# Token sums written unrounded by ScalarE, two modulation vectors moved to VectorE, in a two-layer mLSTM / SGU / conv backbone

## The chip, the cores and the metric

The kernel runs on one core of one Trainium2 chip. The metric is the device time of one execution in microseconds (us). The core has a matrix engine (TensorE, PE in the profile), a vector engine (VectorE, DVE), a scalar engine (ScalarE, ACT), GpSimd (POOL) and a queue engine that issues DMAs (SyncE, SP). Each engine works through its own list of instructions in order and waits on semaphores for the others. Matrix products are accumulated in PSUM, which has eight banks here (the kernel calls them `ps`).

## The reference

The reference is a backbone of two layers over 512 latent tokens and 256 context tokens with 1024 features. Cut to what matters here:

```
for l in range(2):
    mod  = silu(c)     @ w_mod[l] + b_mod[l]      # six vectors: sh1, sc1, g1, sh2, sc2, g2
    modc = silu(c_ctx) @ w_mod[l] + b_mod[l]      # the same for the context tokens
    p = (rmsnorm(x, norm1_g) * (1 + sc1) + sh1) @ w_in[l] + b_in[l]
    y = concat(mlstm(p), spatial_gating(p), conformer_conv(p))
    x = x + g1 * (y @ w_out[l])
    h = rmsnorm(x, norm2_g) * (1 + sc2) + sh2     # "the second norm"
    gate, up = split(h @ w_gu[l])
    x = x + g2 * ((silu(gate) * up) @ w_down[l])
out = rmsnorm(x, final_g)
```

The context tokens go through the same weights with their own modulation; in the second layer only what the latent tokens read of them is computed.

## The kernel before

**Data.** Activations stand with features on the 128 partitions: `xT[:, k, t]` is feature block k (of 8) and token t. Every large product is made from three passes of a rounded format (fp32r): each operand is split into a rounded part `hi`, written by ACT, and the remainder `lo`, written by DVE, and PE adds hi x hi, hi x lo and lo x hi. `HH[:, 0]` and `HH[:, 1]` hold the `hi` and `lo` of the normalised activations.

**Weights.** SP loads 512 KB tiles into four `raw` buffers, in the order in which the program uses them. ACT and DVE split a weight tile (lines 374, 376, 457, 334), and the raw buffer is free after that. A tile of modulation weights is not split; it is free when the engine that uses it is done with it.

**Modulation vectors.** There are two ways to make one of the six vectors of a layer. `mod_steps` makes a vector in eight steps on PE: each step multiplies a 512 KB tile with the two conditioning columns in four matmuls with 32 output rows and 256 columns (line 650). `modh_steps` makes it in two halves of four steps on DVE: each step multiplies two blocks of 512 columns by a conditioning value per partition and adds them up (`macc`; line 724 the first, line 727 the others), for each of the two conditioning columns, four operations per tile; at the end of a half PE sums over the partitions (line 737: eight matmuls, recorded as 16). Both end in `mod_fin`, which transposes the result. Before, layer 0 makes vectors 2, 3, 4 and 5 by `mod_steps`, and layer 1 makes all of its six by `modh_steps` while layer 0's feed-forward part runs. Vector 2 is the gate of the first residual, 3 and 4 are the shift and the scale of the second norm.

**The second norm.** `norm` forms `nt`, the normalised and scaled row of block k, on DVE (line 893); `norm_lo` adds the shift: ACT writes `hi` (line 868), DVE writes `lo` (line 870). It goes through k = 0 to 7, for one group of tokens after the other (layer 0: context 256, latent 512; layer 1: latent 256 and 256).

**The feed-forward part.** The hidden columns of the gate and up projections are made in two ways. The first two (layer 0) or three (layer 1) hidden blocks are "plain" columns: `tiles` over all eight k, with three passes (lines 528 to 530). All the others come as pairs by one level of a fast 2 x 2 product: seven products of quarter size (`pair_steps`, lines 1889 to 1891, PSUM tiles `bA`, `bB`, `bC`) in place of eight. Each product multiplies a combination of weight quarters (formed on DVE, line 420) with a quarter of the activations or with one of four combinations of its quarters, the **token sums**. The activations' quarters are blocks 0 to 3 and 4 to 7 by the first and second half of the tokens. `t_forms` makes the token sums, for k = 0 to 3: it waits for the norm's rows k and k + 4, adds `hi` and `lo` back together into a buffer `tf` (line 1783, 1536 or 1024 columns), combines the quarters in four operations (lines 1786 to 1792), and splits the result again on ACT (line 1796) and DVE (line 1798). There are two `tf` buffers, so that k = 2 and 3 wait for k = 0 and 1. The first pair's second product of activations uses all four token sums.

**Memory.** Twelve `slot` buffers serve the mLSTM part, the convolution, the gating and then the feed-forward part. `ffn_memory` waits for all twelve and hands out the `tf` buffers, the places of the split token sums and places for hidden blocks.

**The order of the work.** The program is written as threads, and a planner (`Plan`) runs them once when the kernel is built: each thread asks for an engine with an estimated cost, and the planner gives each engine to the thread that could start first, on a tie the one with the smaller priority number. The order in which it hands out the engines is the order of each engine's instructions; on the chip it is fixed. PE's list follows the list of steps, into which `spread` mixes modulation steps evenly. Weight splits have priority 0, the norm 0.5, the token sums 0.55 to 0.58, hidden rows 0.6, mLSTM work 0.9 to 3, the convolution's taps and the additions of `modh_steps` 4.

Of the kernel before, what the change touches and what calls it, by code (L numbers as in the profile page):

```python
# [168 lines left out]
def W(ev):  # L169
    return ("w", ev)  # L170
# [53 lines left out]
def backbone(ctx, tc, xT_d, cT_d, wmod_d, wb_d, wgv_d, wv_d, wout_d, wgu_d, wd_d, sw_d, sb_d, cv_d, rv_d, id_d, mk_d, out_d):  # L224
# [639 lines left out]
    def norm_lo(tag, l, which, t, k, grp):  # L864
        n, t0, g, h, o = grp["n"], grp["t0"], grp["g"], grp["h"], grp["off"]
        sh = MODC[l][:, (0, 3)[which], k, g:g + 1]
        yield ACT(n)
        act.activation(h[:, 0, k, o:o + n], t, AF.Identity, bias=sh)
        yield STT(n)
        dve.scalar_tensor_tensor(h[:, 1, k, o:o + n], t, sh, h[:, 0, k, o:o + n].bitcast(F32), ALU.add, ALU.subtract)  # L870
        release("pb")
        fire(ev("h", l, which, t0, k))

    def norm(l, which, grp, stat=None):
# [11 lines left out]
        for k in range(KD):  # L886
# [7 lines left out]
            if k == KD - 1:  # L894
                release("slot" if early else "ps")
# [26 lines left out]
    def layer(l):  # L922
# [765 lines left out]
        if not last:  # L1688
            steps = steps[:first] + spread(steps[first:], [m for v in (2, 3, 4) for m in mod_steps(l, v)])
# [29 lines left out]
        nout = len(steps)  # L1719
# [11 lines left out]
        def spawn_ffn():  # L1731
            spawn(ffn_memory(), 0.5)
            spawn(t_forms(), 0.55)
            return
            yield
# [16 lines left out]
        def ffn_memory():  # L1752
            yield A("slot", 12)
            st["tf"] = [slot([P, 2, 2, HM], "tf") for _ in range(2)]
            sl = [slot([P, 3, 512], "ffn", F32R) for _ in range(10)]
            flat = [x.rearrange("p a b -> p (a b)") for x in sl]
            if not last:
                for k in range(4):
                    TF[k] = tuple(flat[2 * k + w].rearrange("p (a t) -> p a t", a=4) for w in range(2))
                more_hid([tuple(flat[8 + i][:, w * NT:(w + 1) * NT].rearrange("p (a b) -> p a b", a=2) for w in range(2)) for i in range(2)])  # L1760
            else:
                for k in range(4):
                    TF[k] = (HB[:, k // 2, 4 * (k % 2):4 * (k % 2) + 4, :], flat[k][:, 0:1024].rearrange("p (k t) -> p k t", k=4))
                more_hid(piece_hid([x[:, 2] for x in sl[0:4]] + [x[:, i] for x in sl[4:] for i in range(3)]))
# [5 lines left out]
        def t_forms():  # L1770

            yield W(E("ffnmem"))
            tf = st.pop("tf")

            def form(k, f):
                for g in (gl, gg):
                    for kk in (k, k + 4):
                        yield W(ev("h", l, 1, g["t0"], kk))
                if k >= 2:
                    yield W(E("T", k - 2))  # L1780
                rows = [HH[:, w, :, 0:NT].rearrange("p (a b) t -> p a b t", a=2)[:, :, k] for w in range(2)]
                yield DVE2(4 * HM)
                dve.tensor_tensor(f.rearrange("p a b t -> p a (b t)"), rows[0].bitcast(F32), rows[1].bitcast(F32), ALU.add)
                fire(E("tread", k))
                yield DVE2(HM)
                dve.tensor_tensor(f[:, 0, 0], f[:, 0, 0], f[:, 0, 1], ALU.subtract)
                yield DVE2(HM)
                dve.tensor_tensor(f[:, 0, 1], f[:, 1, 1], f[:, 0, 1], ALU.subtract)
                yield STT(HM)
                dve.scalar_tensor_tensor(f[:, 1, 1], f[:, 0, 0], -1.0, f[:, 1, 1], ALU.mult, ALU.subtract)  # L1790
                yield STT(HM)
                dve.scalar_tensor_tensor(f[:, 1, 0], f[:, 1, 1], -1.0, f[:, 1, 0], ALU.mult, ALU.subtract)
                hi, lo = TF[k]
                ff = f.rearrange("p a b t -> p (a b) t")
                yield ACT(4 * HM)
                act.copy(hi, ff)
                yield DVE2(4 * HM)
                dve.tensor_tensor(lo, ff, hi.bitcast(F32), ALU.subtract)  # L1798
                fire(E("T", k))
                if k >= 2:  # L1800
                    release("slot")

            for k in range(4):
                spawn(form(k, tf[k % 2]), 0.55 + 0.01 * k)
            yield W(E("T", 2))
            yield W(E("T", 3))
            yield A("slot", 2)
            x = [slot([P, 3, 512], "ffn", F32R) for _ in range(2)]
            if not last:
                x = [y.rearrange("p a b -> p (a b)") for y in x]  # L1810
                more_hid([tuple(y[:, w * NT:(w + 1) * NT].rearrange("p (a b) -> p a b", a=2) for w in range(2)) for y in x])
            else:
                more_hid(piece_hid([y[:, i] for y in x for i in range(3)]))
# [6 lines left out]
        def more_room():  # L1820
            for k in range(4):
                yield W(E("tread", k))
# [258 lines left out]
        steps.append(([], lambda: spawn_ffn()))  # L2081
        np_ = NPLAIN[l]
        steps += tiles([gu_col(i) for i in range(2 * np_)], gl, gg, KD, hsrc, lambda k, g: ev("h", l, 1, g["t0"], k), wide=True, ahead=AHEAD[2])
# [176 lines left out]
```

## Time and profile before

The device time is 1557.0 us, the median of three runs from 1554.63 to 1558.24. The profile is of one further execution.

| | before |
|---|---|
| time of the profiled execution | 1559.97 us |
| its span, first to last instruction | 1558.1 us |
| PE busy | 1503.7 us, 97% |
| PE weight loads busy | 1396.0 us, 90% |
| DVE busy | 1119.8 us, 72% |
| ACT busy | 675.1 us, 43% |
| POOL busy | 32.9 us, 2% |
| mean granted TensorE clock | 0.99 |
| moved by DMA | 173.24 MB, 111 GB/s |

Times in rows of the profile count from the start of the span. A row of the timeline is: start, duration, engine, line of the kernel, operation, what is written <- what is read, shape, count, and in brackets the idle time of the engine just before it with what ended it. PE rows overlap, since matmuls are pipelined: the distance of two starts is the time that a matmul takes from the stream. PEld is PE's loading of the stationary operand. SPq is the queue in which SP issues DMAs.

### The profile page before, as it was taken

How to read it: one execution, taken by the hardware profiler on the slowest of the kernel's cores; microseconds unless marked ns; L12 is line 12 of the kernel's file. 1: busy time of each engine (PE TensorE's matmuls, PEld its weight loads, DVE VectorE, ACT ScalarE, POOL GpSimd, SP SyncE). 2: the span in 40 equal slices, each digit the busy share in tenths (PEclk: the TensorE clock that was granted, in tenths of full speed). 3: DMA queues.
4: the chain of work that ended last, by engine and by line, in shares of the span. 5: the costliest groups of instructions: out<-in, count | busy, mean ns of one | idle time of the engine just before them, and what ended most of it. 6: DMA issues, size and time to landing. Idle time of an engine off the chain costs nothing.

```text
span 1558.1 us, 26164 instructions
## 1 busy us (share of the span) xinstructions
PE 1503.7 (97%) x10276; PEld 1396.0 (90%) x10276; DVE 1119.8 (72%) x2372; ACT 675.1 (43%) x1395; POOL 32.9 (2%) x50
## 2 busy tenths in 40 slices
PE   5999999999989999999999999999999999999997
PEld 4887778888889999999999998878999999999997
DVE  4459966464898887777777775496767986877865
ACT  4332266642443333333433443416664554544534
POOL 0000000000000000000000000000000000000000
PEclk9999999999999999999999999999999999999999
DMA  9333245323224323343343431312332233332331
GB/s 329 136 122 126 73 154 157 123 76 102 81 81 137 107 101 129 116 142 111 119 133 100 140 103 57 104 58 95 109 109 69 73 105 96 103 106 92 107 102 63
DMA packets 71800, 173.24 MB, mean 111 GB/s; under 512 B 7565, under 2 KB 19965, under 8 KB 71677
## 3 DMA queue, kind: packets, MB, share of 16 engines
q1 hardware_dynamic: 68908, 170.16, 34.0%
q8 instruction: 80, 1.31, 0.3%
q10 hardware_dynamic: 2768, 1.42, 0.3%
q14 instruction: 44, 0.35, 0.1%
HBM read 169.34 MB, written 2.21 MB: 110 GB/s over the span
## 4 chain that ended last, share of the span: by engine, by line
PE 73%; DVE 16%; DMA 6%; issue 3%; ACT 2%; POOL 0%; SPq 0%; POOLq 0%; DVEq 0%; ACTq 0%
PE mm L528 13%; PE mm L529 13%; PE mm L530 13%; PE bA L1889 4%; PE bA L1890 4%; PE bA L1891 4%; DVE lo L376 3%; DMA raw<-in_wgu 2%; PE bC L1889 2%; PE bC L1890 2%; PE bC L1891 2%; DMA raw<-in_wd 2%; DVE macc L727 2%; DVE raw L420 1%; PE vp L1304 1%
## 5 line engine op out<-in xcount | busy, mean ns | idle before, releaser
L528 PE MATMUL mm<-HH,hi 128*128 128x256 f32 (+2 forms) x1040 | 351.3, 338 | 0.3 <-ACT HH L1603 0.3
L529 PE MATMUL mm<-HH,hi 128*128 128x256 f32 (+2 forms) x1040 | 338.1, 325 | 5.4 <-DVE HH L870 4.3
L530 PE MATMUL mm<-HH,lo 128*128 128x256 f32 (+2 forms) x1040 | 337.8, 325 | 0.2 <-DVE lo L334 0.2
L374 ACT CAST hi<-raw 128x512 fp32r<-128x512 f32 (+2 forms) x361 | 209.8, 599 | 251.0 <-PE mm L529 59.6
L376 DVE TENSOR_TENSOR lo<-raw,hi 128x512 fp32r<-128x512 f32 (+2 forms) x361 | 228.6, 658 | 30.2 <-ACT hi L374 27.2
L528 PEld LDWEIGHTS mm<-HH,hi 128*128 128x128 f32 x1040 | 197.4, 190 | 23.6 <-issue 10.7
L529 PEld LDWEIGHTS mm<-HH,hi 128*128 128x128 f32 x1040 | 197.9, 190 | 17.7 <-DVE HH L870 5.2
L530 PEld LDWEIGHTS mm<-HH,lo 128*128 128x128 f32 x1040 | 197.1, 190 | 15.3 <-DVE lo L334 0.4
L528 PE MATMUL mm<-ffn,hi 128*128 128x256 f32 (+1 forms) x576 | 177.1, 307 | 1.8 <-ACT hi L374 1.8
L530 PE MATMUL mm<-ffn,lo 128*128 128x256 f32 (+1 forms) x576 | 176.3, 306 | 0.0
L529 PE MATMUL mm<-ffn,hi 128*128 128x256 f32 (+1 forms) x576 | 176.2, 306 | 0.0
L334 DVE TENSOR_TENSOR lo<-raw,hi 128x1024 fp32r<-128x1024 f32 (+4 forms) x92 | 102.3, 1120 | 83.4 <-ACT hi L457 79.0
L2028 DVE SCALAR_TENSOR_TENSOR xT<-mm,modc,xT 128x256 f32<-128x256 f32 (+2 forms) x208 | 95.9, 479 | 80.5 <-PE mm L530 80.1
L1890 PE MATMUL bA<-ffn,hi 128*128 128x384 f32 (+1 forms) x468 | 145.7, 311 | 3.3 <-DVE ffn L1798 3.3
L457 ACT CAST hi<-raw 128x1024 fp32r<-128x1024 f32 (+4 forms) x92 | 87.8, 964 | 132.6 <-PE mm L529 49.8
L420 DVE TENSOR_TENSOR raw<-raw 128x512 f32<-128x512 f32 x156 | 103.6, 685 | 27.0 <-DMA raw<-in_wgu 25.8
L1889 PE MATMUL bA<-HH,hi 128*128 128x256 f32 (+1 forms) x384 | 112.2, 292 | 3.6 <-ACT x L1963 3.1
L1891 PE MATMUL bA<-HH,lo 128*128 128x256 f32 (+1 forms) x384 | 112.0, 292 | 0.0
L528 PEld LDWEIGHTS mm<-ffn,hi 128*128 128x128 f32 x576 | 108.5, 188 | 2.8 <-ACT hi L374 2.1
L530 PEld LDWEIGHTS mm<-ffn,lo 128*128 128x128 f32 x576 | 108.6, 189 | 0.5 <-DVE lo L376 0.4
L529 PEld LDWEIGHTS mm<-ffn,hi 128*128 128x128 f32 x576 | 108.7, 189 | 0.0
L1890 PEld LDWEIGHTS bA<-ffn,hi 128*128 128x128 f32 x468 | 88.1, 188 | 4.1 <-DVE ffn L1798 4.1
(263 smaller groups left out, 2966.7 us busy)
## 6 DMA issues: line engine op xcount, KB each, us to landing
raw<-in_wmod SPq DMA_DIRECT2D x96, 512.0 KB, 3.8
raw<-in_wgu SPq DMA_DIRECT2D x88, 512.0 KB, 3.7
raw<-in_wb SPq DMA_DIRECT2D x36, 512.0 KB, 3.6
pbt<-dr SPq DMA_DIRECT2D x40, 256.0 KB, 3.6
raw<-in_wd SPq DMA_DIRECT2D x40, 256.0 KB, 2.7
raw<-in_wout SPq DMA_DIRECT2D x16, 512.0 KB, 3.6
raw<-in_wd SPq DMA_DIRECT2D x16, 384.0 KB, 3.1
raw<-in_wd SPq DMA_DIRECT2D x16, 320.0 KB, 2.9
```

Of the source, the lines that this page charges most:

```text
L334: dve.tensor_tensor(lo, r, hi.bitcast(F32), ALU.subtract)
L374: act.copy(hi, x)
L376: dve.tensor_tensor(lo, x, hi.bitcast(F32), ALU.subtract)
L420: dve.tensor_tensor(o, x, y, op)
L457: act.copy(hi, RAW[i])
L528: pe.matmul(o, lhsT=hi[:, k, :], rhs=hh, start=(j == 0), stop=False)
L529: pe.matmul(o, lhsT=hi[:, k, :], rhs=hl, start=False, stop=False)
L530: pe.matmul(o, lhsT=lo[:, k, :], rhs=hh, start=False, stop=(j == nk - 1))
L1889: pe.matmul(o, lhsT=hi[:, k], rhs=rh, start=start and k == 0, stop=False, skip_group_check=True)
L1890: pe.matmul(o, lhsT=hi[:, k], rhs=rl, start=False, stop=False, skip_group_check=True)
L1891: pe.matmul(o, lhsT=lo[:, k], rhs=rh, start=False, stop=k == 3, skip_group_check=True)
L2028: dve.scalar_tensor_tensor(x, p[:, a - h["t0"]:b - h["t0"]], MODC[l][:, 5, d, g["g"]:g["g"] + 1], x, ALU.mult, ALU.add)
```

## The change

1. **Unrounded rows.** `t_forms` and its adding back of `hi` and `lo` are gone. For the second norm, a new thread `norm_copy` has ACT write the shifted row a second time, unrounded, straight into the buffer in which the token sum is formed (`FORM`, four of them, one for each k of 0 to 3). The buffer `nt` is released when both are done. `norm_copy` waits for `ffn_memory`.
2. **Pair order.** The second norm goes through the blocks in the order 0, 4, 1, 5, 2, 6, 3, 7, and the plain columns use them in that order.
3. **Memory.** `ffn_memory` is spawned ahead of the output projection, not at the start of the feed-forward part; it gives four slots to `FORM`, some to hidden blocks, and releases the rest, from which the split token sums take theirs one by one. In layer 0 it first waits until vector 4's second half has its slot.
4. **Modulation.** Vectors 2 and 4 of layer 0 are made by `modh_steps` on DVE. Vector 2's steps are spread over the first seven steps after the k columns, vector 4's over the last 14 steps ahead of the output projection, and vector 3's, still on PE, in between.

```
         yield ACT(n)
         act.activation(h[:, 0, k, o:o + n], t, AF.Identity, bias=sh)
+        left = [2 if which else 1]
...
+        if which:
+            spawn(norm_copy(l, t, sh, k, grp, done), S.cur.prio)
         yield STT(n)
         dve.scalar_tensor_tensor(h[:, 1, k, o:o + n], t, sh, h[:, 0, k, o:o + n].bitcast(F32), ALU.add, ALU.subtract)
-        release("pb")
+        done()
         fire(ev("h", l, which, t0, k))
+    KORDER = (0, 4, 1, 5, 2, 6, 3, 7)
+    def norm_copy(l, t, sh, k, grp, done):
+        n, t0 = grp["n"], grp["t0"]
+        yield W(ev(l, "ffnmem"))
+        yield ACT(n)
+        act.activation(FORM[l, k % 4][:, k // 4, t0:t0 + n], t, AF.Identity, bias=sh)
+        done()
+        fire(ev("hf", l, t0, k))
...
         if not last:
-            steps = steps[:first] + spread(steps[first:], [m for v in (2, 3, 4) for m in mod_steps(l, v)])
+            a, b, c = first + 7, len(steps) - 14, len(steps) - 0
+            steps = (steps[:first] + spread(steps[first:a], modh_steps(l, 2)) + spread(steps[a:b], [m for v in (3,) for m in mod_steps(l, v)])
+                     + spread(steps[b:c], [m for v in (4,) for m in modh_steps(l, v)]) + steps[c:])
...
+        def ffn_memory():
+            if not last:
+                yield W(ev("macc", 0, 4, 1))
+            n = 5 if not last else 1
+            yield A("slot", 12)
+            for k in range(4):
+                FORM[l, k] = slot([P, 4 * HM], "tf").rearrange("p (a t) -> p a t", a=2)
+            hid_slots([slot([P, 3, 512], "ffn", F32R) for _ in range(8 - n)])
+            release("slot", n)
+            fire(E("ffnmem"))
...
+        def t_form(k):
+            for g in (gl, gg):
+                for kk in (k, k + 4):
+                    yield W(ev("hf", l, g["t0"], kk))
+            ff = FORM.pop((l, k)).rearrange("p a (b t) -> p (a b) t", b=2)
+            b11, b12, b21, b22 = (ff[:, i] for i in range(4))
...
+            yield ACT(4 * HM)
+            act.copy(hi, ff)
+            yield DVE2(4 * HM)
+            dve.tensor_tensor(lo, ff, hi.bitcast(F32), ALU.subtract)
+            fire(E("T", k))
+            release("slot")
...
-        steps.append(([], lambda: spawn_ffn()))
+        steps.insert(nffn, ([], lambda: spawn_ffn()))
-        steps += tiles([gu_col(i) for i in range(2 * np_)], lambda k, g: ev("h", l, 1, g["t0"], k), wide=True, ahead=AHEAD[2])
+        steps += tiles([gu_col(i) for i in range(2 * np_)], lambda k, g: ev("h", l, 1, g["t0"], k), KORDER, wide=True, ahead=AHEAD[2])
```

More of the change, by code (lines that the diff above doesn't have):

```diff
@@ L885, in norm @@
             rb = r
-        for k in range(KD):
+        for i, k in enumerate(KORDER if which else range(KD)):
             yield W(ev("gs", l, which, k))
@@ L893, in norm @@
             dve.scalar_tensor_tensor(t, xT[:, k, t0:t0 + n], gs[:, k, g:g + 1], rb, ALU.mult, ALU.mult)
-            if k == KD - 1:
+            if i == KD - 1:
                 release("slot" if early else "ps")
@@ L1718, in layer @@
         steps.append(spawn_gs(l, 1))
-        nout = len(steps)
+        nout = nffn = len(steps)
         steps += tiles([out_col(d) for d in range(KD)], gl, gg, KD, hsrc, lambda k, g: E("ys", g["t0"], k), YK, wide=True, ahead=AHEAD[1])
@@ L1732, in spawn_ffn @@
             spawn(ffn_memory(), 0.5)
-            spawn(t_forms(), 0.55)
+            for k in range(4):
+                spawn(t_form(k), 0.55 + 0.01 * k)
             return
@@ L1750, in piece_hid, with hid_slots @@
             return list(zip(p[0::2], p[1::2]))
[L1752 to L1755, printed above, removed]
+        def hid_slots(sl, parts=3):
             flat = [x.rearrange("p a b -> p (a b)") for x in sl]
             if not last:
[L1758 to L1764, printed above, removed]
+                more_hid([tuple(x[:, w * NT:(w + 1) * NT].rearrange("p (a b) -> p a b", a=2) for w in range(2)) for x in flat])
+                return
+            spare = st.setdefault("pieces", [])
+            spare += [x[:, i] for x in sl for i in range(3 - parts, 3)]
+            n = len(spare) // 2 * 2
+            more_hid(piece_hid(spare[:n]))
+            del spare[:n]
+        def ffn_memory():
[3 more added lines that the diff above has]
+            yield A("slot", 12)
+            for k in range(4):
+                FORM[l, k] = slot([P, 4 * HM], "tf").rearrange("p (a t) -> p a t", a=2)
+            hid_slots([slot([P, 3, 512], "ffn", F32R) for _ in range(8 - n)])
+            release("slot", n)
             fire(E("ffnmem"))
@@ L1768, in quarter @@
             return HH[:, which, 4 * kh:4 * kh + 4, th * HM:(th + 1) * HM]
[L1770 to L1808, printed above, removed]
@@ L1809, in t_forms @@
             if not last:
-                x = [y.rearrange("p a b -> p (a b)") for y in x]
-                more_hid([tuple(y[:, w * NT:(w + 1) * NT].rearrange("p (a b) -> p a b", a=2) for w in range(2)) for y in x])
-            else:
-                more_hid(piece_hid([y[:, i] for y in x for i in range(3)]))
+                yield A("slot", 2)
+                hi, lo = (slot([P, 4, HM], "T", F32R) for _ in range(2))
+            else:
+                yield A("slot")
+                x = slot([P, 3, 512], "T", F32R)
+                hi = HB[:, k // 2, 4 * (k % 2):4 * (k % 2) + 4, :]
+                lo = x.rearrange("p a b -> p (a b)")[:, 0:1024].rearrange("p (k t) -> p k t", k=4)
@@ L1815, in plain_done @@
+            TF[k] = hi, lo
+            yield ACT(4 * HM)
[4 more added lines that the diff above has]
+            release("slot")
+            if last:
+                hid_slots([x], 1)
+            st["nT"] = st.get("nT", 0) + 1
+            if st["nT"] == 4:
+                yield A("slot")
+                hid_slots([slot([P, 3, 512], "ffn", F32R)])
         def plain_done():
@@ L1820, in more_room @@
         def more_room():
-            for k in range(4):
-                yield W(E("tread", k))
+            yield W(E("ffnmem"))
             more_hid([tuple(HH[:, w, 2 * i:2 * i + 2, HM:2 * HM] for w in range(2)) for i in range(2)], "hh" if not last else "hp")
@@ L2079, in t_free @@
             yield
-        steps.append(([], lambda: spawn_ffn()))
+        steps.insert(nffn, ([], lambda: spawn_ffn()))
         np_ = NPLAIN[l]
-        steps += tiles([gu_col(i) for i in range(2 * np_)], gl, gg, KD, hsrc, lambda k, g: ev("h", l, 1, g["t0"], k), wide=True, ahead=AHEAD[2])
+        steps += tiles([gu_col(i) for i in range(2 * np_)], gl, gg, KD, hsrc, lambda k, g: ev("h", l, 1, g["t0"], k), KORDER, wide=True, ahead=AHEAD[2])
         if not last:
```

13 lines of the change are left out of this document (added).

## The prediction

> **What bounds the kernel now.** I read the page first, then the table of busy time by stretch, then the matmuls one after another around each place where they fall out of step.
>
> ```profile
> span 1558.1 us, 26164 instructions
> PE 1503.7 (97%) x10276; PEld 1396.0 (90%) x10276; DVE 1119.8 (72%) x2372; ACT 675.1 (43%) x1395; POOL 32.9 (2%) x50
> ```
>
> PE is busy for all but 54 us of the span. Busy alone does not say that it streams at its best, so here is a stretch of layer 1's feed-forward part and one of layer 0's (columns: stretch, then busy time and instructions of PE, weight loads, DVE, ACT, POOL, the granted clock, DMA share, GB/s).
>
> ```profile
> 450.00:460.00 10.00, 10.00 (x59) 10.00 (x59) 7.11 (x13) 5.07 (x10) 0.00 (x0) 1.00 0.57 196
> 1400.00:1500.00 100.00, 100.00 (x852) 100.00 (x851) 77.69 (x148) 49.01 (x98) 0.00 (x0) 1.00 0.33 102
> ```
>
> 59 matmuls of 384 columns start in 10 us, one in 0.17 us; 852 of 256 columns in 100 us, one in 0.117 us. I call this the pitch. PE keeps it for whole stretches with no gap, so a matmul that leaves PE takes its pitch out of the end time, and elsewhere only places that lose pitch can give anything. The change works on both.
>
> **Part 1: two modulation vectors leave PE.** Vectors 2 and 4 of layer 0 take 8 steps each of line 650 today. One such step on PE:
>
> ```profile
> 80.83 0.29 PE L978 MATMUL gvp<-lo,HH 128*128 128x272 f32 x1
> 80.96 0.29 PE L979 MATMUL gvp<-hi,HH 128*128 128x272 f32 x1
> 81.18 0.64 PE L650 MATMUL modps<-raw,csil 128*32 128x256 f32 x8
> 81.75 0.39 PE L977 MATMUL gvp<-hi,HH 128*128 128x272 f32 x1
> 81.98 0.28 PE L978 MATMUL gvp<-lo,HH 128*128 128x272 f32 x1
> ```
>
> From 80.96 to 81.98 two neighbours start, which need 2 x 0.13 (80.83 to 80.96); 1.02 - 0.26 leaves 0.76 us for the step. 16 steps: 12.2 us. What comes in are four halves of line 737, each 16 recorded matmuls for the two conditioning columns, as layer 0's feed-forward part already runs for layer 1:
>
> ```profile
> 516.70 0.33 PE L1891 MATMUL bA<-ffn,lo 128*128 128x384 f32 x1
> 516.97 0.65 PE L737 MATMUL modps<-macc,esel 128*32 128x128 f32 x16
> 517.54 0.45 PE L1889 MATMUL bA<-ffn,hi 128*128 128x384 f32 x1
> 517.82 0.34 PE L1890 MATMUL bA<-ffn,hi 128*128 128x384 f32 x1
> ...
>   DVE macc L727: 2.8, 6
> ```
>
> 1.12 - 2 x 0.17 = 0.78 us each, 3.1 us for four. The final transposes stay the same in number (two of 128 columns per vector). So PE gets **-9.1 us**. The last row, from the view of line 737, says that PE and its weight loads together waited 2.8 us in six of twelve such blocks for the additions; at worst each of the four waits 2.8 / 6 = 0.5 us, so the term lies between -9.1 and -7.1. I take -9.1: in the quoted block nothing waits.
>
> **Part 2: what DVE takes over.** A half vector is 2 multiplications (line 724) and 14 multiply-adds (line 727), which now come from these rows, and the large additions of line 1783 go (columns of the grouped view: shapes and count, then busy us and mean ns).
>
> ```profile
> L724 DVE TENSOR_SCALAR macc<-raw,csil 128x512 f32<-128x512 f32 x16 | 7.5, 478 | 0.0
> L727 DVE SCALAR_TENSOR_TENSOR macc<-raw,csil,macc 128x512 f32<-128x512 f32 x112 | 81.8, 745 | 0.7
> L1783 DVE TENSOR_TENSOR tf<-HH 128x1536 f32<-128x1536 f32 x4 | 6.9, 1748 | 0.0
> L1783 DVE TENSOR_TENSOR tf<-HH 128x1024 f32<-128x1024 f32 x4 | 4.8, 1212 | 0.0
> ```
>
> Each half costs 2 x 0.478 + 14 x 0.745 = 11.4 us, each vector 22.8, both 45.6; 11.7 go. DVE's share rises from 1120 to about 1154 us, still far under PE's. What counts is where it falls.
>
> ```profile
> 80.00:100.00 20.00, 20.00 (x165) 17.42 (x165) 5.59 (x21) 4.50 (x6) 0.00 (x0) 1.00 0.39 118
> 100.00:200.00 100.00, 97.80 (x589) 76.53 (x589) 92.86 (x235) 32.87 (x63) 5.01 (x9) 0.98 0.31 104
> 260.00:335.00 75.00, 74.94 (x515) 64.09 (x514) 44.29 (x126) 48.36 (x119) 4.18 (x6) 1.00 0.38 120
> ```
>
> Vector 2 is spread over the first seven steps from the gv slabs on, about 80 to 115 us. DVE is idle for 14.4 of the 20 us to 100, so some 14 us of the 22.8 are covered by idleness; the other 8 land where DVE is 93% busy, and its lowest-priority work (convolution taps, the same priority as these additions) slides by about 8 us, into the 7 us still free before 200 and the looser stretch behind. The gates, the weight splits and the v evacuation have better priority, so they wait for one running addition (0.75 us) at most each time. Vector 4 falls into the last 14 steps before the output projection, about 260 to 335: DVE has 30.7 us free there for 22.8. Were these covers gone, the price would be 22.8 us of DVE at each place.
>
> PE's own waits in 80 to 335 are small, the longest entry being this:
>
> ```profile
> PE hT L1565 <- DVE hacc L1560: 3.0, 2, 1.6
> ```
>
> Fuller holes should make such waits grow. Bounds: 0 if all fits, +22.8 if vector 4 stood wholly ahead of the mLSTM outputs that the projection needs. Nearest is the free end, since the holes are wider than the work: I take **+3**, a doubling of that row.
>
> **The loads.** The bytes are unchanged, 16 tiles of 512 KB, but eight now crowd into about 35 us and a raw tile is free only after four additions (3 us), not after PE's 0.76. All loads go through SP's queue in order, behind them the row broadcasts of line 1465. What that queue waited for (total, times, longest), first between 60 and 400 us, then the whole span:
>
> ```profile
> SPq L328 <- PE modps L650: 136.1, 26, 16.0
> ...
> SPq L328 <- DVE macc L727: 175.6, 37, 13.2
> ```
>
> So the loader already waits up to 16 us for a tile that PE must free here, and elsewhere up to 13.2 for one held by additions. One kind replaces the other; I cost it at nothing, covered by the split weights that stand ahead of PE, and keep the rest for a rival.
>
> **Part 3: the start of layer 0's pairs.** Here PE loses the most:
>
> ```profile
> 433.79 0.34 PE L1891 MATMUL bB<-HH,lo 128*128 128x384 f32 x1
> 436.09 0.44 PE L1889 MATMUL bA<-ffn,hi 128*128 128x384 f32 x1 [1.96 <-ACT x L1963]
> ...
> 438.08 0.63 PE L1890 MATMUL bA<-ffn,hi 128*128 128x384 f32 x1 [0.51 <-DVE ffn L1798]
> 438.51 0.53 PE L1891 MATMUL bA<-ffn,lo 128*128 128x384 f32 x1
> 438.83 0.53 PE L1889 MATMUL bA<-ffn,hi 128*128 128x384 f32 x1
> 442.15 0.69 PE L1890 MATMUL bA<-ffn,hi 128*128 128x384 f32 x1 [2.80 <-DVE ffn L1798]
> ...
> 445.99 0.34 PE L1889 MATMUL bA<-ffn,hi 128*128 128x384 f32 x1
> ```
>
> 13 matmuls of this chain (bB's last and 12 of bA) and 12 of bC start between 433.79 and 445.99: 25 x 0.17 = 4.3 of 12.2 us, so 7.9 us are lost. The named releaser of the main wait is the rounding remainder of a token sum (line 1798); the first wait is a copy standing behind a token-sum cast in ACT's queue.
>
> ```profile
> 400.00:448.00 48.00, 42.73 (x227) 36.31 (x226) 47.97 (x73) 24.10 (x38) 0.00 (x0) 0.93 0.13 44
> 440.35 1.75 DVE L1798 TENSOR_TENSOR ffn<-tf,ffn 128x1536 fp32r<-128x1536 f32 x1
> ```
>
> DVE is full from 400 to 448. The last remainder ends at 442.1. With four additions of 1.75 fewer ahead of it, it would end at 435.1 even in the old order; the third and fourth sum also no longer wait for a buffer of the first two, and pair order lets sum 0 start after two of the eight norm rows, not five. PE's last of the four needs comes at 433.96 + 10 x 0.17 = 435.7, so the remainder is in time by a hair in the old order and easily in the new. ACT's casts move ahead too, so its copy is not stuck. Of 7.9 I take **-7** (bounds -7.9 and 0, the latter if another DVE piece takes the place).
>
> The gap has a clock part: after the waits bA's matmuls come 0.32 us apart (438.51 to 438.83), not 0.17. The Trainium skill's page "TensorE: Matmul & The Clock Gate", section "What's actually happening", says the clock halves after an idle window of about 3.4 us. By that rule a wait merely cut below a window would free the whole slow stretch; the rows show the slow pitch already at 438.51, before the 3 us wait and after two shorter ones, so a remnant could still slow it. As I forecast both waits gone, the term is the same by either; with a remnant of 2 us the row would make it about -5, the rule about -6.
>
> **Part 4: the same place in layer 1**, and what its norm gets:
>
> ```profile
> 1231.81 0.28 PE L1891 MATMUL bB<-HH,lo 128*128 128x256 f32 x1
> 1235.21 0.39 PE L1889 MATMUL bA<-HH,hi 128*128 128x256 f32 x1 [3.13 <-ACT x L1963]
> 1235.44 0.28 PE L1890 MATMUL bA<-ffn,hi 128*128 128x256 f32 x1
> ...
> 1197.00:1232.00 35.00, 34.81 (x295) 34.49 (x293) 34.82 (x67) 19.92 (x37) 0.87 (x1) 1.00 0.11 36
> PE mm L529 <- DVE HH L870: 1.7, 2, 1.0
> L868 ACT ACTIVATE HH<-nt,modc 128x256 fp32r<-128x256 f32 x40 | 19.2, 506 | 20.8 <-DVE nt L893 20.4 <-PE mm L530 0.3
> L868 ACT ACTIVATE HH<-nt,modc 128x512 fp32r<-128x512 f32 x24 | 17.2, 723 | 18.9 <-DVE nt L893 18.5
> ```
>
> 3.63 us for two pitches of 0.117: 3.4 lost, ACT's copy queued behind a cast that waits for a DVE backlog. DVE is full (34.82 of 35) and loses 4 x 1.21 = 4.8 us of work. I take **-2.5** (bounds -3.4 and 0).
>
> The new unrounded copies are ACT's: 8 of 0.506 and 8 of 0.723 in layer 0, 16 of 0.506 in layer 1, 18 us in all. ACT is half idle there (24.1 of 48, 19.9 of 35). Each stands between two rounded rows in ACT's queue, and the row that DVE subtracts from comes one copy later at most. The third row above, from 1190 to 1200, is where PE waits on that chain in layer 1; two waits, each later by up to two copies, is +2. I take **+0.5** of 0 to +2. The copies also wait for 12 free slots; the last of these come free when the y rows are split, and the whole output projection stands between that and the norm, so this wait I cost at nothing. Behind it, were it late, stand the four norm buffers and with them the norm.
>
> **The sum.** -9.1 + 3 - 7 - 2.5 + 0.5 = -15.1 us. The profiled execution took 1559.97 us in all (1558.1 of span), so it would take 1544.9. That execution stood 3.0 us above the median of the runs, 1557.0; on the median it gives **1542 us**.
>
> **The rivals.**
> - *The backlog moves on* (chance 13%). DVE stays full from 400 to 448 and 1197 to 1232, and behind the sums stand weight splits and hidden rows; PE then waits for those. Against: seven of 48 us of DVE work really go. Without the -7 and -2.5: -5.6, 1551 us.
> - *PE had slack where the matmuls leave* (11%). If mLSTM or DVE sets the pace from 80 to 335, the freed 9.1 us turn into waits there. For: 97.80 of 100 busy and DVE at 92.86. Against: 74.94 of 75 busy. Then about -6, 1551 us.
> - *Both, or the change does not do what it says on the path* (8%): -15.1 + 9.1 + 7 + 2.5 - 3 = about 0, 1557 us.
> - *SP's queue* (10%), the slower one. In 255 to 335 the row broadcasts, vector 4's tiles and the projection's weights stand in one queue. A tile held by low-priority additions blocks the broadcasts behind it, the mLSTM outputs come late, the additions with them. Two waits of 13.2 us, one per half, are 26.4 us. It decides from 18.1 us on, the gain without the +3. For: the 13.2 row. Against: waits of 16.0 stand on this queue now, and PE lost 3.0 to its chain. Uncovered: -18.1 + 26.4 = +8.3, 1565 us.
>
> **How the numbers follow.** The forecast has 58%, with its own range 1536 to 1547: all of the gaps and no new waits (-9.1 - 7.9 - 3.4 = -20.4) to the additions costing some 5 us more. A measurement of this kernel cannot tell a change under 0.2% (3 us) from none. Faster: 58 + 13 + 11 = 82%; same 8%; slower 10%. The range 1534 to 1556 holds the forecast and the first two rivals and leaves out most of the last two.
>
> **What would show it.** Right: line 650 with 128 instead of 256 recorded matmuls and line 737 with 192 instead of 128; no waits above 1 us for the token sums at the first pairs of either layer, the granted clock at 1.00 there; DVE busy in 80 to 100 raised to near 20, in 260 to 335 to about 67; waits of PE in 80 to 335 within some 3 us more. Wrong: PE waiting at the same pairs for weight splits (first rival), PE idle grown between 80 and 335 by as much as the matmuls freed (second), SP waiting more than 13 us for additions with the broadcasts behind, and PE for the output projection (last).

## The result, and the profile after

| | median us | lowest to highest | runs |
|---|---|---|---|
| before | 1557.6 | 1554.6 to 1559.6 | 4 |
| after | 1538.2 | 1534.9 to 1540.7 | 4 |

The changed kernel takes 0.987 of the time before (95% interval 0.9851 to 0.9888), 19.4 us less by the medians (that of before, 1557.0 above, has one more run here). The forecast was 1542 us in a range of 1534 to 1556. The two profiled executions differ by more, 1558.1 to 1533.1 us of span. The one of before lies 2.4 us above its median (1559.97 us), the one of after 3.3 below its own (1534.92), so 5.6 of the 25.0 us are spread between runs, and stretches of the traces have to be compared, not the ends.

From the page of after:

```profile
span 1533.1 us, 26131 instructions
PE 1488.5 (97%) x10212; PEld 1390.5 (91%) x10212; DVE 1147.0 (75%) x2430; ACT 686.0 (45%) x1428; POOL 33.7 (2%) x50
```

PE is busy 15 us less, DVE 27 more, ACT 11 more. For DVE the forecast had 34, from the means of its groups; additions in a row overlap in the records (nine of 0.74 us within 6.30 us, from 70.18 us of the second profile below), so the busy time grows by less. Then the views of lines 650 and 737 (count, shortest, median and longest ns, first and last start; in the third row us and times that line 737 waited for line 727) and the group of line 727 (busy us and mean ns):

```profile
L650 PE MATMUL modps<-raw,csil x128: 379/391/404, 109.8 to 412.3; 128*32 128x256 f32 x128
L737 PE MATMUL modps<-macc,esel x192: 272/273/297, 96.0 to 879.1; 128*32 128x128 f32 x192
  DVE macc L727: 4.7, 7
```

```profile
L727 DVE SCALAR_TENSOR_TENSOR macc<-raw,csil,macc 128x512 f32<-128x512 f32 x168 | 122.3, 743 | 0.8
```

128 matmuls of line 650 instead of 256, 192 of line 737 instead of 128, 168 multiply-adds instead of 112, at the price that they had before. Waits of line 737 for the additions grew from 2.8 to 4.7 us.

The table by stretch, after (columns as before):

```profile
80.00:100.00 20.00, 20.00 (x155) 18.50 (x154) 9.47 (x30) 1.88 (x4) 0.00 (x0) 1.00 0.25 79
100.00:200.00 100.00, 96.31 (x591) 75.71 (x589) 96.74 (x235) 32.53 (x62) 1.98 (x4) 1.00 0.41 125
200.00:260.00 60.00, 57.88 (x404) 51.45 (x405) 50.89 (x169) 41.26 (x128) 7.65 (x11) 1.00 0.43 137
260.00:335.00 75.00, 75.00 (x497) 66.58 (x496) 57.67 (x145) 45.86 (x117) 4.55 (x6) 1.00 0.34 107
400.00:448.00 48.00, 47.20 (x252) 42.95 (x251) 45.50 (x78) 25.80 (x46) 0.00 (x0) 1.00 0.24 77
```

From 400 to 448 PE starts 252 matmuls where it started 227, at a granted clock of 1.00 instead of 0.93. The waits of PE in 400 to 460 and then in 1130 to 1260 (total, times, longest):

```profile
PE bA L1912 <- ACT x L1986: 0.8, 1, 0.8
...
PE mm L529 <- DVE HH L879: 1.7, 2, 1.0
```

The waits of 2 and 2.8 us at the first pairs of layer 0 are down to one of 0.8, and that of 3.1 us in layer 1 is gone; the norm's two waits of layer 1 are what they were, to the tenth. SP's queue between 60 and 400 us:

```profile
SPq L328 <- PE modps L650: 46.0, 11, 10.6
SPq L1486 <- PE num L1549: 25.2, 11, 5.2
SPq L328 <- DVE macc L727: 22.3, 6, 12.7
```

It waits 22 us for tiles that additions hold, but no longer 136 for tiles that PE holds, and its row broadcasts (line 1486 now) wait 5.2 us at the most.

To compare stretches I take four starts of matmuls from each trace: the norm 2's first sum in layer 0 (line 831), the last bA of the pairs of layer 0, and the same two in layer 1. The first column below is from the span's start to the first of them, the others lie between two starts, so that they hold nothing of the noise ahead. For before it is 380.8, 886.2, 1186.6 and 1502.3 us. The experiments below are in the table already.

```
                              to norm 2   norm 2 + pairs   between   norm 2 + pairs   median
                               layer 0       layer 0                    layer 1         us
before                          380.8         505.4          300.4       315.7        1557.6
after, first profile            369.5         495.1          301.0       311.7        1538.2
after, second profile           373.3         495.1          299.1       311.7        1537.0
modulation alone                373.8         504.3          299.4       317.1        1555.1
token sums alone                376.2         496.0          301.9       311.3        1543.5
vector 2 alone on DVE           373.1         496.2          301.2       311.7        1538.9
rows in order 0 to 7            373.0         495.2          301.7       311.7        1539.2
additions back                  372.0         503.3          299.1       316.9        1549.5
both of these                   373.1         502.4          301.8       317.9        1551.9
copies twice                    371.9         500.1          300.5       314.2        1543.6
vector 3 on DVE too             377.8         494.7          303.1       311.2        1544.1
vector 5 on DVE at the pairs    370.1         508.7          300.8       311.8        1548.2
vector 5 in the projection      381.0         495.1          300.8       311.6        1542.5
```

The second and fourth columns are steady to about 1.5 us between kernels with the same code there; the first varies by about 4 us (before and the token sums alone run the same up to the norm: 380.8 and 376.2).

### The profile page after: what moved, and what is told of

Its sections match the earlier page's. It is cut to its first block, busy times and chain, and to the rows that moved or that the text cites. A ratio compares the mean times of both kernels' runs of the same rounds, so it can differ in the third digit from the quotient of the medians.

```text
span 1533.1 us, 26131 instructions
## 1 busy us (share of the span) xinstructions
PE 1488.5 (97%) x10212; PEld 1390.5 (91%) x10212; DVE 1147.0 (75%) x2430; ACT 686.0 (45%) x1428; POOL 33.7 (2%) x50
## 4 chain that ended last, share of the span: by engine, by line
PE 81%; DVE 11%; DMA 4%; ACT 2%; issue 2%; POOL 0%; SPq 0%; POOLq 0%; DVEq 0%; ACTq 0%
PE mm L528 14%; PE mm L529 14%; PE mm L530 14%; PE bA L1912 5%; PE bA L1913 5%; PE bA L1914 5%; PE bC L1912 2%; PE bC L1913 2%; PE bC L1914 2%; DVE lo L376 1%; DMA raw<-in_wgu 1%; DVE lo L334 1%; PE bB L1912 1%; PE vp L1325 1%; PE bB L1913 1%
## 5 line engine op out<-in xcount | busy, mean ns | idle before, releaser
L528 PE MATMUL mm<-ffn,hi 128*128 128x256 f32 (+1 forms) x544 | 167.4, 308 | 0.0
L529 PE MATMUL mm<-ffn,hi 128*128 128x256 f32 (+1 forms) x544 | 167.0, 307 | 0.0
L530 PE MATMUL mm<-ffn,lo 128*128 128x256 f32 (+1 forms) x544 | 166.7, 307 | 0.1
L1913 PE MATMUL bA<-T,hi 128*128 128x384 f32 (+1 forms) x468 | 145.4, 311 | 0.0
L727 DVE SCALAR_TENSOR_TENSOR macc<-raw,csil,macc 128x512 f32<-128x512 f32 x168 | 122.3, 743 | 0.8
L420 DVE TENSOR_TENSOR raw<-raw 128x512 f32<-128x512 f32 x156 | 103.8, 686 | 23.6 <-DMA raw<-in_wgu 22.8
L528 PEld LDWEIGHTS mm<-ffn,hi 128*128 128x128 f32 x544 | 102.3, 188 | 0.8 <-issue 0.6
L530 PEld LDWEIGHTS mm<-ffn,lo 128*128 128x128 f32 x544 | 102.2, 188 | 0.4 <-DVE lo L376 0.4
L529 PEld LDWEIGHTS mm<-ffn,hi 128*128 128x128 f32 x544 | 102.3, 188 | 0.0
```

What stands on the lines that cost most here:

```text
L420: dve.tensor_tensor(o, x, y, op)
L528: pe.matmul(o, lhsT=hi[:, k, :], rhs=hh, start=(j == 0), stop=False)
L529: pe.matmul(o, lhsT=hi[:, k, :], rhs=hl, start=False, stop=False)
L530: pe.matmul(o, lhsT=lo[:, k, :], rhs=hh, start=False, stop=(j == nk - 1))
L727: dve.scalar_tensor_tensor(a[g], s[:, i, :], c, a[g], ALU.mult, ALU.add)
L1913: pe.matmul(o, lhsT=hi[:, k], rhs=rl, start=False, stop=False, skip_group_check=True)
```

## The experiments

The experiments ran on three chips. The runs of before beside them have medians of 1557.6 to 1558.2 us, so times of different chips are compared as they are.

**1. The two halves of the change by themselves.** Modulation alone, on the kernel before:

```
-            steps = steps[:first] + spread(steps[first:], [m for v in (2, 3, 4) for m in mod_steps(l, v)])
+            a, b, c = first + 7, len(steps) - 14, len(steps) - 0
+            steps = (steps[:first] + spread(steps[first:a], modh_steps(l, 2)) + spread(steps[a:b], [m for v in (3,) for m in mod_steps(l, v)])
+                     + spread(steps[b:c], [m for v in (4,) for m in modh_steps(l, v)]) + steps[c:])
```

> The kernel before with the modulation vectors 2 and 4 of layer 0 on DVE and nothing else changed; everything is still computed. My theory: PE is the bound between 80 and 335 us, so it gains the 16 steps of 0.76 us less four blocks of 0.78 us, 9.1 us, and the additions on DVE cost nothing, since the trace after shows no new waits of PE there: 1557.6 - 9.1 = 1548.5 us; the first statistic of norm 2 comes 8 to 10 us earlier than in before, 380.8, and the stall at the first pairs stays, 433.8 to 446.0 shifted by as much, about 8 us lost. The forecast's +3 for contention: 1551.5 us and the statistic only 6 us earlier. Rival, PE had slack there: no more than 3 us gained, 1554.6 or more, and the 11.4 us by which that statistic came earlier in the changed kernel came from elsewhere.

Measured: 1555.1 us against 1558.1, ratio 0.9983 (0.9972 to 0.9995). Token sums alone, on the changed kernel:

```
-            a, b, c = first + 7, len(steps) - 14, len(steps) - 0
...
+            steps = steps[:first] + spread(steps[first:], [m for v in (2, 3, 4) for m in mod_steps(l, v)])
...
-            if not last:
-                yield W(ev("macc", 0, 4, 1))
```

> The changed kernel with vectors 2 and 4 back on PE, so that only the unrounded copies, the token sums in their place and the order of rows are new; everything is still computed. My theory: the two stalls at the first pairs go (7.9 us in layer 0, 3.5 in layer 1) and two small ones that followed in layer 0 (1.9 and 1.7 us), with nothing paid in the norm: 11 to 15 us less than before, 1543 to 1546.5; the first statistic of norm 2 stays at 380 +- 2 us. Forecast's own terms -7 - 2.5 + 0.5: 1548.6. Rival, the stall went because the modulation work came earlier and the backlog only moves on here: no more than 3 us gained, PE waiting again at the first pairs.

Measured: 1543.5 us, ratio 0.9908 (0.9895 to 0.9922), 14.5 us less. Waits of PE in 410 to 460, modulation alone and then token sums alone:

```profile
PE bA L1892 <- DVE ffn L1800: 3.3, 2, 2.8
PE bA L1891 <- ACT x L1965: 2.0, 1, 2.0
```

```profile
PE bA L1908 <- ACT x L1982: 0.7, 1, 0.7
```

So the stalls go with the token sums and not with the earlier modulation: three quarters of the whole gain. In the table they take 505.4 to 496.0 in layer 0 and 315.7 to 311.3 in layer 1, 13.8 us. The modulation by itself came out between the theories. Its trace reaches norm 2 7.0 us earlier than that of before, between my 8 to 10 and the forecast's 6, but only 2.4 us earlier than that of the token sums alone, which runs the same as before up to there; its median is the rival's, 3.0 us less. On top of the token sums it brings more, from 1543.5 to 1538.2 or 1537.0, 5.3 to 6.5 us.

**2. What about the token sums removed the stalls?** The forecast held that it was DVE's time, with the new order of rows as a help. Two edits and both together, on the changed kernel:

```
-    KORDER = (0, 4, 1, 5, 2, 6, 3, 7)
+    KORDER = tuple(range(8))
```

> The changed kernel with the eight rows of norm 2, and the columns of the plain products behind it, in the order 0 to 7 again; everything is still computed. The first token sum can then start after row 4, the last after row 7 as before. The forecast's theory, the DVE time of the four large additions is what removed the stalls: the last remainder is in time by a hair in the old order, 1538 to 1541 us. Rival, the pair order (the early start) is what removed them: the waits for the remainder are back at the first pairs, 1544 us or more.

```
             b11, b12, b21, b22 = (ff[:, i] for i in range(4))
+            yield DVE2(4 * HM)
+            dve.tensor_tensor(ff, ff, ff, ALU.max)
```

> The changed kernel with one DVE instruction more ahead of each token sum, which takes the larger of each number and itself and so changes nothing but puts back the size of the old large additions, 4 x 1.75 us in layer 0 and 4 x 1.21 in layer 1; everything is still computed. Forecast's theory, DVE's time is what counts: part of the stalls is back, 3 to 9 us in layer 0 and 1 to 3 in layer 1, 1542 to 1549 us, with PE waiting for the remainder of a token sum. Rival, the order and the four buffers are what counts: 1537 to 1540 us, no such wait.

> The two edits together: rows in the order 0 to 7 and the DVE instruction of the old additions' size ahead of each token sum; everything is still computed. What is left of the part on the token sums is the ACT copies and that no sum waits for another's buffer. If DVE's time and the order are the whole of it: 1550 to 1555 us, the time of the kernel with only the modulation moved (1555.1), with PE waiting some 8 us at the first pairs of layer 0 and 3 in layer 1. If the buffers or the earlier casts on ACT matter by themselves: 1543 to 1549 us.

Measured: 1539.2 (ratio 0.9888, 0.9870 to 0.9906), 1549.5 (0.9950, 0.9933 to 0.9966) and 1551.9 us (0.9967, 0.9955 to 0.9980). The order is worth nothing that these runs can tell. With the additions back: the added instructions (groups), the remainders of layer 0's token sums (line 1831), PE's waits at the first pairs of each layer, and the stretch:

```profile
L1810 DVE TENSOR_TENSOR tf<-tf 128x1536 f32<-128x1536 f32 x4 | 7.0, 1750 | 0.0
...
L1810 DVE TENSOR_TENSOR tf<-tf 128x1024 f32<-128x1024 f32 x4 | 4.9, 1216 | 0.0
```

```profile
L1831 DVE TENSOR_TENSOR T<-tf,T x4: 1750/1751/1752, 409.8 to 430.4; 128x1536 fp32r<-128x1536 f32 x4
```

```profile
PE bA L1914 <- ACT x L1988: 5.7, 1, 5.7
...
PE bA L1914 <- ACT x L1988: 3.5, 1, 3.5
```

```profile
400.00:448.00 48.00, 42.34 (x208) 37.64 (x208) 47.03 (x73) 23.66 (x41) 0.00 (x0) 0.93 0.19 58
```

And the remainders in the changed kernel:

```profile
L1829 DVE TENSOR_TENSOR T<-tf,T x4: 1750/1751/1758, 403.1 to 419.3; 128x1536 fp32r<-128x1536 f32 x4
```

There the last one starts at 419.3 us, when the first bA has just begun (418.5); with the additions back it starts at 430.4, 9 us behind the first bA (421.0); in before it was at 440.4, 11 us behind (429.8). DVE got 4 x 1.750 + 4 x 1.216 = 11.9 us of work, and the end came 11.3 us later than 1538.2 (12.5 later than 1537.0). The first matmuls of the pairs lose what they lost before: in layer 0 their 49th matmul starts 16.2 us behind the first bA in before, 16.3 with the additions back and 8.4 in the changed kernel. DVE is busy all of 395 to 415 even in the changed kernel, and the 11.9 us put there and at the same place of layer 1 cost about as much of the whole (8.2 us in layer 0's stretch of the table, 5.2 in layer 1's). The stretch from 400 to 448 shows the clock at 0.93 again, as before the change. With the order taken back too, the time is still 3.2 us short of that of the modulation alone (1555.1), whose token sums are the old ones; by the stretches of both layers the two differ by 1.1 us. What the copies on ACT and the four buffers bring by themselves is within that, and wasn't taken apart.

**3. What does ACT's copy cost?**

```
         act.activation(FORM[l, k % 4][:, k // 4, t0:t0 + n], t, AF.Identity, bias=sh)
+        yield ACT(n)
+        act.activation(FORM[l, k % 4][:, k // 4, t0:t0 + n], t, AF.Identity, bias=sh)
```

> The changed kernel with each of the 32 unrounded copies of ACT written twice, 18 us more on ACT in the two norms; everything is still computed. The forecast's +0.5 us (0 to +2) for one set of copies: 1538.2 to 1540.2 us here, no new wait of PE in the norms. Rival, ACT's copies already stand on the path of the norm: two rows in a row come later by two copies each, +3 us or more, 1541 us or more, with the wait of the plain products for the DVE half of a row grown above its 1.0 us.

Measured: 1543.6 us, ratio 0.9915 (0.9896 to 0.9934): the rival's time. The table puts 5.0 us into layer 0 and 2.5 into layer 1. Stretches of layer 0's norm in the changed kernel's second profile (ACT is the fourth pair):

```profile
385.00:395.00 10.00, 9.97 (x89) 9.36 (x88) 5.79 (x10) 3.98 (x7) 1.01 (x1) 1.00 0.51 171
395.00:405.00 10.00, 10.00 (x65) 8.45 (x65) 10.00 (x17) 9.78 (x16) 0.00 (x0) 1.00 0.19 54
```

And with the copies twice, a matmul, a stretch and a wait:

```profile
388.16 1.05 PE L831 MATMUL stat<-onesD,acc 128*128 128x1 f32 x8 [1.38 <-DVE acc L781]
390.00:395.00 5.00, 5.00 (x35) 5.00 (x35) 1.45 (x3) 0.66 (x2) 0.50 (x1) 0.73 0.24 91
PE modT L623 <- ACT modsb L617: 1.0, 1, 1.0
```

One set of copies fills ACT for the 10 us in which the long rows of 512 tokens go through (9.78 of 10). A second set fills it already in the short rows of 256 tokens ahead of them (5.00 of 5 us from 380 to 385). There a weight split and the latent tokens' squares stand behind the copies in ACT's queue, PE waits 1.38 us for the sum of the squares, and behind the wait the granted clock is down (0.73 in the stretch, 1.00 in the changed kernel), which by the distances of the matmuls costs some 1.4 us more. With the wait of 1.0 us these make the 3.9 us that are lost ahead of the first bA. So the rival's path, plain products waiting for the DVE half of a row, is not what cost the time: that wait grew only from 1.0 to 1.2 us, in layer 1. The first set of copies was free as far as PE shows it (from the norm's first sum to the first bA layer 0 takes 49.0 us in before and after, and 52.9 with two sets), the second cost 5 to 7: the cover is just used up. That ACT is half idle over the longer stretch, on which the forecast rested, does not show it.

**4. How much more can DVE take?** Vector 5 at the first pairs, vector 3 ahead of the projection, vector 4 back on PE, and vector 5 in the projection:

```
-            steps = steps[:nout] + spread(steps[nout:], mod_steps(0, 5))
...
+            cut5 = nfirst + (len(steps) - nfirst) // 12
+            steps = (steps[:nfirst] + spread(steps[nfirst:cut5], modh_steps(0, 5, "wi"))
...
```

> The changed kernel with vector 5 of layer 0 also on DVE, moved from the second half of the output projection to the first twelfth of the pairs of layer 0, ahead of layer 1's vectors; everything is still computed. PE loses 8 steps of 0.76 us and gets two blocks of 0.78: -4.5 us, 1533.7 us, if DVE, busy 7 of 10 us there, takes 22.8 us more within about 40 us. Rival: DVE's splits and rows for the first pairs come late, PE waits for them as it did before the change: 1538 us or more.

```
-            a, b, c = first + 7, len(steps) - 14, len(steps) - 0
+            a, b, c = first + 7, len(steps) - 22, len(steps) - 0
+            steps = (steps[:first] + spread(steps[first:a], modh_steps(l, 2)) + steps[a:b]
+                     + spread(steps[b:c], [m for v in (3, 4) for m in modh_steps(l, v)]) + steps[c:])
```

> The changed kernel with vector 3 of layer 0 on DVE as well, its two halves and vector 4's spread over the last 22 steps ahead of the output projection; everything is still computed. It puts 22.8 us more on DVE ahead of the norm and takes 8 x 0.76 - 2 x 0.78 = 4.5 us from PE. If DVE's additions only fill holes: 1538.2 - 4.5 = 1533.7 us. If the holes are full by now (before had 30.7 us free in 260 to 335 and vector 4 took 22.8): some of the 22.8 comes out as waits of PE for DVE, and the time is 1538 to 1556 us.

Measured: 1548.2 (ratio 0.9936, 0.9924 to 0.9949) and 1544.1 us (0.9912, 0.9898 to 0.9927), slower than the changed kernel by 10.0 and 5.9, though PE has 4.5 us less to do in each. Waits of PE with vector 5 at the pairs (410 to 460), then with vector 3 too, the longest rows of 80 to 335 and the two stretches:

```profile
PE bA L1914 <- DVE lo L376: 3.7, 1, 3.7
PE bA L1912 <- ACT x L1986: 1.5, 1, 1.5
```

```profile
PE hT L1586 <- DVE hacc L1581: 5.1, 3, 2.4
PE mm L530 <- DVE lo L334: 3.6, 4, 1.5
```

```profile
200.00:260.00 60.00, 54.05 (x387) 48.31 (x386) 57.78 (x192) 35.11 (x126) 7.84 (x10) 0.97 0.44 133
260.00:335.00 75.00, 70.23 (x463) 61.28 (x462) 61.96 (x149) 48.23 (x109) 6.83 (x8) 0.98 0.41 130
```

The first brings back the forecast's first rival by hand: PE waits at the pairs for the remainder of a weight split (line 376). 22.8 us of DVE's lowest priority cost 10 us net there, 14.5 without what PE saves. In the second, DVE is 57.78 of 60 us busy (50.89 in the changed kernel) and PE waits for its chain through line 1581: 5.9 us net, 10.4 without the saving.

Vector 4 back on PE:

```
-            a, b, c = first + 7, len(steps) - 14, len(steps) - 0
...
+            a, b = first + 7, len(steps)
+            steps = (steps[:first] + spread(steps[first:a], modh_steps(l, 2)) + spread(steps[a:b], [m for v in (3, 4) for m in mod_steps(l, v)]))
...
-            if not last:
-                yield W(ev("macc", 0, 4, 1))
```

> The changed kernel with vector 4 of layer 0 back on PE, vector 2 alone on DVE; everything is still computed. Each vector is worth 8 x 0.76 - 2 x 0.78 = 4.5 us of PE. If only the first window (DVE 93 of 100 us busy before) is contended, vector 2 has brought about 1.5 and vector 4 its 4.5: 1542 to 1543 us, close to the kernel with both on PE (1543.5). If only the second window is contended, or neither: vector 2 has brought its 4.5, 1539 to 1540 us, and vector 4 the rest.

> The changed kernel itself once more, as the measure for the two others on the same chip: 1538 +- 1.5 us. Its first profile (1534.9 us) was its fastest run; if that was luck in the clock and the start, the first statistic of norm 2 comes 2 to 4 us later this time than 369.5, with the same stalls.

Measured on one chip: 1538.9 us (ratio 0.9874, 0.9854 to 0.9895) and 1537.0 (0.9862, 0.9843 to 0.9881). By the medians vector 2 brings all of its 4.5 us (1543.5 to 1538.9) and vector 4 only 1.9, so that the contention, 2.6 us, would all be vector 4's; since the intervals of these two overlap, that share isn't settled. The traces point the same way: all waits of PE from 80 to 335 us add up to 5.7 and 4.3 us with both vectors on PE (before, token sums alone), to 4.0 with vector 2 alone on DVE, and to between 5.1 and 8.0 in the eight profiles with both there. The longest wait of PE from 200 to 335, in the changed kernel and then with vector 2 alone, is one for DVE in the first and for ACT in the second:

```profile
PE num L1546 <- DVE pbt L1499: 2.0, 1, 2.0
```

```profile
PE hT L1586 <- ACT pbt L1496: 1.1, 1, 1.1
```

The last one puts vector 5 where DVE was half idle:

```
-            steps = steps[:nout] + spread(steps[nout:], mod_steps(0, 5))
+            steps = steps[:nffn] + spread(steps[nffn:nout], modh_steps(0, 5, "wi")) + steps[nout:]
```

> The changed kernel with vector 5 of layer 0 on DVE in the first half of the output projection, where DVE was busy for 29.3 of the 60 us from 320 to 380; everything is still computed. The same 22.8 us of DVE that cost 10 us net at the first pairs fall into a hole here. If the place decides: 1538.2 - 4.5 = 1533.7 us and no stall at the first pairs. Rival, the loads of its weights or its two buffers hold up the projection or the norm's sums of squares: 1538 us or more, with PE waiting between 335 and 400.

Measured: 1542.5 us (1537.6 to 1546.1), ratio 0.9889 (0.9867 to 0.9910). This interval overlaps that of the changed kernel, two of the six runs were as fast as it, and the trace is that of the slowest, so it shows what can go wrong here and not the price. From the norm's first sum to the end of layer 0's pairs the time is the same (495.1 us): 3.6 us less up to the first bA, where modulation steps have left PE, and as much more behind it. The way to the norm is longer. SP's wait for additions from 296 to 303 us, its issues and PE's matmuls at the projection's start, with vector 5 there:

```profile
SPq L328 <- DVE macc L727: 7.0, 1, 7.0
```

```profile
285.62 9.57 SPq L328 DMA_DIRECT2D raw<-in_wmod  x2
302.25 7.16 SPq L328 DMA_DIRECT2D raw<-in_wout  x2
```

```profile
321.09 0.39 PE L528 MATMUL mm<-HH,hi 128*128 128x256 f32 x1 [1.59 <-ACT hi L457]
321.31 0.28 PE L529 MATMUL mm<-HH,hi 128*128 128x256 f32 x1
322.71 0.58 PE L530 MATMUL mm<-HH,lo 128*128 128x256 f32 x1 [1.11 <-DVE lo L334]
323.08 0.41 PE L528 MATMUL mm<-HH,hi 128*128 128x256 f32 x1
323.30 0.41 PE L529 MATMUL mm<-HH,hi 128*128 128x256 f32 x1
...
328.57 0.28 PE L530 MATMUL mm<-HH,lo 128*128 128x256 f32 x1
328.69 0.28 PE L528 MATMUL mm<-HH,hi 128*128 128x256 f32 x1
```

Two modulation tiles are issued ahead of the projection's weights (the first row spans both issues and the wait between them, which the view does not put down to additions). The first projection tile then waits 7.0 us until additions free a buffer: it is issued at 302.25 us, in the changed kernel's second profile at 284.22, and PE waits for splits of such tiles. That is the queue of the forecast's slower rival, called up by one vector more, with the projection's weights held up instead of the row broadcasts. No version beat the changed kernel.

## Why the prediction was right, step by step

**The total.** 1542 forecast, 1538.2 measured: the sum was -15.1, the medians give -19.4. The direction and the mechanism of both halves held; the difference of 4 us lies in the token sums.

**PE's matmuls, -9.1, and DVE's additions, +3.** Together -6.1; measured -5.3 to -6.5 on top of the token sums, -3.0 (0.8 to 4.4) alone. The counts of lines 650 and 737 are as forecast; the four new blocks of line 737 took 3.9 us out of the stream, not 3.1 (0.78, 1.48, 0.85 and 0.77 by the starts around them). The contention's size held by the medians, though PE's waits from 80 to 335 us show only some 1.4 us of it (means of the profiles in experiment 4) and the dearer blocks 0.8. Its place did not hold: vector 4 starts at 228.9 us, not 260, so DVE rose in 200 to 260 to 50.89 and in 260 to 335 only to 57.67, not to 67. And vector 2, of whose work the working had 8 us land where DVE is 93% busy, cost nothing: it starts at 68.5 us, not 80, and 23 of its 32 instructions on DVE begin ahead of 100 us, where DVE is half idle (9.47 of 20 us busy from 80 to 100, not near 20 as forecast; the starts are from the second profile of the changed kernel). Why the modulation alone gave some 3 us less than on top of the token sums is open: its trace doesn't lose them at the pairs of layer 0 (504.3 against 505.4), and of layer 1 it shows only 1.4 (317.1 against 315.7).

**Layer 0's pairs, -7.** Measured -9.4 (505.4 to 496.0), with the modulation -10.3, beyond the bound of -7.9. The step mis-sized is "25 x 0.17 = 4.3 of 12.2 us, so 7.9 us are lost": it counted one place. Two further waits in before, some 45 and 130 us later, went as well:

```profile
489.00 0.44 PE L528 MATMUL mm<-ffn,hi 128*128 128x384 f32 x1 [1.78 <-ACT hi L374]
...
575.59 0.45 PE L1889 MATMUL bA<-ffn,hi 128*128 128x384 f32 x1 [1.56 <-ACT x L1963]
```

The first belongs to the backlog. It stands at 1.69 us with the modulation alone, and with the additions back it is there again:

```profile
480.27 0.44 PE L528 MATMUL mm<-ffn,hi 128*128 128x384 f32 x1 [1.71 <-ACT hi L374]
```

The second does not: with the modulation alone, where the token sums are the old ones, and with the additions back PE has no wait of this kind from 445 to 700 us, while the token sums alone still show one of 0.94. What took it away is open. With the main stall's 7.9 the first makes 9.7, close to the 9.4 of the token sums alone. Of the two reasons given, DVE's time is shown (experiment 2) and the order of rows is not: the sentence that it "lets sum 0 start after two of the eight norm rows" is true and moves nothing, since DVE is full either way.

**Layer 1's pairs, -2.5.** Measured -4.0 to -4.4 (315.7 to 311.7 and 311.3), a little past the bound of -3.4; the stall of 3.4 is wholly gone.

**ACT's copies, +0.5.** Measured 0, but with less to spare than the half idle ACT of the forecast: twice the copies cost 5 to 7 us. **The loads, 0:** right for two vectors, and at the edge: a third vector's tiles, out of place, brought out the delay of the slower rival.

**The rivals.** PE had no slack where vector 2's matmuls leave; where vector 4's leave, new waits for DVE took part of the gain back, by the medians, and that is the contention. The backlog did not move on; it does when DVE gets 11.9 or 22.8 us more there (experiments 2 and 4).

**The clock.** The granted clock from 400 to 448 went from 0.93 to 1.00 as forecast, with no remnant of a wait to test the rule of the Trainium skill's page "TensorE: Matmul & The Clock Gate".

## What to carry to other kernels

Look for the stretch in which a helping engine is full to the end of a stage that PE then needs: there its work is worth its whole duration (11.9 us of DVE cost 11.3), while the same work elsewhere is worth a fraction of it or nothing. Take an engine's idleness over the 5 or 10 us in which its work falls, not over 50: ACT was 25.80 of 48 us busy, and yet a second set of copies filled it for 5.00 of 5 us where the squares stood behind them. And price a stall with the waits that follow out of the same backlog, here one of 1.8 us.

## What the runs showed of the hardware that was not expected

Waits well under 3 us halved the clock. In the last experiment PE waited 1.59 and 1.11 us, and behind them its matmuls of 256 columns came 0.22 us apart (323.08 to 323.30) instead of 0.12 (328.57 to 328.69). Stretches there, then one behind the wait of 3.5 us in layer 1 with the additions back, then one around the wait of 3.13 us in before:

```profile
322.00:324.00 2.00, 1.29 (x6) 1.30 (x7) 2.00 (x5) 0.48 (x2) 0.00 (x0) 0.50 0.10 8
326.00:328.00 2.00, 2.00 (x12) 2.00 (x11) 0.98 (x3) 0.00 (x0) 0.00 (x0) 0.50 0.00 0
```

```profile
1225.00:1230.00 5.00, 5.00 (x36) 5.00 (x35) 3.19 (x5) 2.44 (x5) 0.00 (x0) 0.77 0.00 0
```

```profile
1231.00:1236.00 5.00, 1.87 (x16) 1.67 (x15) 5.00 (x13) 2.48 (x6) 0.00 (x0) 1.00 0.53 172
```

The granted clock is 0.50 from 322 to 328, and the 27 matmuls from 322.71 to 328.57 take 2.6 us more than at 0.12 us each, about as much as the two waits themselves. With the copies twice one wait of 1.38 us was enough (experiment 3): it stood between short matmuls, a modulation step of 32 output rows and eight sums of one column, and behind it the matmuls came 0.21 us apart; in the changed kernel the same short matmuls without the wait leave the clock at 1.00. A single wait of 3.5 us between full matmuls brought it down too, one of 3.13 us did not. The Trainium skill's page "TensorE: Matmul & The Clock Gate", section "What's actually happening", gives an idle window of about 3.4 us that runs freely. By the first two cases a window need not be idle throughout; how much of it must be was not tested. The spread of the runs goes with the clock too: of 17 runs of before beside one another the shortest span (1551.0 us) has a mean granted clock of 0.994 and the longest (1558.8) 0.988, and the eight runs of the changed kernel, 1533.1 to 1538.9 us, have clocks from 0.992 to 0.996.
